# A streaming encoder trunk on one Trainium2 core: keys in plain fp32 and a divided norm in the opening

## The chip, the cores and the metric

The kernel runs on one core of a Trainium2 chip. Five engines work side by side, each with its own queue of instructions: TensorE (PE in the profile, and PEld for its loads of stationary weights), VectorE (DVE), ScalarE (ACT), GpSimd (POOL) and SyncE (SP), which here only issues transfers. The metric is the device time of one execution in microseconds (us); a kernel's time is the median of several runs.

## What is computed

One step of an encoder layer with 512 prompt positions and 8 x 16 sample positions, 640 rows of 1024 channels in all. Cut to what the change touches:

```python
xp = layer_norm(x_prompt, ln_in_g, ln_in_b)          # the same for x_sample
mem_k = mem_prompt @ w_mem_k                          # (256, 512): output, and keys of the prompt's attention
mem_v = mem_prompt @ w_mem_v                          # (256, 512): output, and values
z = x @ w_in                                          # 6656 columns: five inputs of three branches
...                                                   # branches a (conv + RG-LRU), b (conv), c (attention)
merged = g0 * out_a + g1 * out_b + g2 * out_c
x = layer_norm(alpha * x + merged @ w_out, ln1_g, ln1_b)
x = layer_norm(alpha * x + ffn(x), ln2_g, ln2_b)
```

All data are float32. `layer_norm` subtracts the row's mean, divides by its standard deviation, multiplies by a weight (g) and adds a bias (b) per channel.

## The kernel before, in words

**Products.** A float32 operand is split into a high part in the type fp32r (a copy on ACT, into tiles named `xh`, `wh`) and the rest (a subtraction on DVE, `xl`, `wl`). A product is then three fp32r matmuls: high x high, high x low, low x high. `split`, lines 199 to 201, does one operand, `split_all`, 203 to 208, several, all copies first. Activations stand turned, channels on partitions: `xh` and `xl` are [128, 8, 640].

**Order.** Everything is unrolled in program order. A list of `Step`s (257 to 303) holds a load of weights, the matmuls and what follows them. The loop at 1865 to 1893 takes them in order: it issues the high copies of the weights one step ahead at the start and two later (`prep_hi`), then the step's matmuls; at each `yield` in these, `advance` (319) lets side jobs, the generators in `streams`, issue instructions while a running sum of estimated prices says that ACT and DVE are ahead of PE, and after it come the waiting evacuations (`flush`, 310) and the low parts of the new weights (`prep_lo`). Each engine does its instructions strictly in that order, so a late one holds up those behind it. Scratch rows on chip are 53 slots, given out in the order in which they came free (`Slots`, 110). PSUM has four single banks (`pu`) and two double ones (`pv`).

**The opening.** Loads go out on SP's queue at lines 427 to 438: memory, key weights, x tile 0, gain and bias of the input norm repeated over 128 rows (`gb_in`, 1 MB), value weights, x tiles 1 and 2; line 1848 on adds x tiles 3 and 4, the first two loads of `w_in` and the rows of parameters (`pa`, `pb`, line 611). PE begins with warm-up matmuls on an identity (`idle`, 560 to 562). Then come eight steps (`mem_steps`, 589), four for the keys and four for the values, each with its half of the memory and one pair of weight blocks, all split. The dictionary `jobs` (584) writes out by hand what is issued after each: the memory's splits (`mem_split`), and for x tiles 0 to 3 statistics (`x_stats`), the norm in four DVE passes over rows (`x_norm`, 521), the turn by eight PE transposes into one `pv` (`x_turn`), the split out of PSUM and the store of the normed rows to the DRAM scratch `xn` (`x_split`, 533). `start_stream` (543) does tile 4 and the last two turns while the first product with `w_in` runs.

**The first product with `w_in`.** Its first three steps are a group (line 667 on): first the columns 0 to 319 of all three, which need x tiles 0 to 2, then columns 320 to 639, which need all five. `fm` (638) issues, for each block of 128 channels, the three products one after the other. Before the second columns `start_over` (700) finishes the stream.

**Later.** Gated products, attention, the recurrent branch; then eight steps of `proj_a` (line 1515), and the product with `w_out`, before which `before_out` (1630) begins to load the normed rows back from `xn` on POOL's queue as the residual (`load_res`, 1543; `x1_sum`, 1560).

Of the kernel before, what the change touches and what calls it, by code (L numbers as in the profile page):

```python
# [11 lines left out]
OP = mybir.AluOpType  # L12
# [131 lines left out]
def trunk(ctx, tc, x_prompt, x_sample, mem_t, rows_a, rows_b, hist_b, cache_k, cache_v, ln_in_g, ln_in_b, w_in,  # L144
# [251 lines left out]
    pa = one.tile([128, KD, 45], F32, name="pa")  # L396
# [3 lines left out]
    scratch = {n: tc.dram_tile([T, D], F32, name=n) for n in ("xn", "x1")}  # L400
# [80 lines left out]

    def to_xt(t, x):

        yield from room()
        p = pv()
        for c in range(2):
            for k in range(4):
                P.transpose(p[:, c, k * 128:(k + 1) * 128], x[c][:, k * 128:(k + 1) * 128], ident)
        yield None
        over()  # L490
        sl = slice(t * 128, (t + 1) * 128)
        split_all([(xh[:, 4 * c:4 * c + 4, sl], xl[:, 4 * c:4 * c + 4, sl], p[:, c].rearrange("p (k n) -> p k n", n=128))
                   for c in range(2)])
        turned.add(t)
        yield 1

# [21 lines left out]
    def x_root(t):  # L518
        norm[t] = ln_root(*norm[t])

    def x_norm(t):
        g, b = gb_in
        mv, ve, rs = norm.pop(t)
        y = xt[t]
        for c in range(2):
            V.scalar_tensor_tensor(y[c], y[c], mv[:, 0:1], g[c], op0=OP.subtract, op1=OP.mult)
            V.scalar_tensor_tensor(y[c], y[c], rs, b[c], op0=OP.mult, op1=OP.add)

    def x_turn(t):
# [13 lines left out]
    def start_stream():  # L543
        x_stats(4)
        yield None
        x_norm(4)
        for t in (3, 4):
            yield None
            yield from room()
            x_turn(t)  # L550
            yield None
            x_split(t)
        for r in gb_in:
            free(*r)

    def mem_end():
        stream("start", start_stream())
        P.time = max(P.time, V.time, A.time)
# [7 lines left out]
    def mem_evac(which):  # L566
# [6 lines left out]
        if which == "k":  # L573
            kv["k"] = out
        else:
            for m in range(2):
                hi, lo = get([128, 512], F32R), get([128, 512], F32R)
                split(hi, lo, out[m])
                vN[m] = (hi, lo)
            free(*out)  # L580
            for x in memT.values():
                free(*x)

    jobs = {0: [(mem_split, 1)], 1: [(mem_split, 2)], 2: [(mem_split, 3), (x_norm, 0)], 3: [(x_turn, 0), (x_stats, 1)],
            4: [(x_norm, 1), (x_split, 0), (mem_evac, "k"), (x_stats, 2)], 5: [(x_turn, 1), (x_norm, 2)],
            6: [(x_split, 1), (x_turn, 2), (x_stats, 3, False)],
            7: [(x_root, 3), (x_split, 2), (mem_evac, "v"), (x_norm, 3), (mem_end,)]}

    def mem_steps(which, li):
        for s in range(4):  # L590
            def mm(w, s=s):
# [12 lines left out]
            Step(mem_w[li + s], lambda r: r, [128, 2, 512], mm)  # L604
# [62 lines left out]
    def x_step(ld, o, evac, group=None):  # L667

        def mm(w):
# [4 lines left out]
            if group[1][0] is s:  # L674
                until(lambda: {0, 1, 2} <= turned)
                for z, q in enumerate(group[1]):
# [3 lines left out]
                    for n, few in enumerate(fm(q.p, q.w, xrh, xrl, KD, (0,))):  # L680
# [828 lines left out]
    for j in range(KD):  # L1509
# [4 lines left out]
                for j in range(0, KD, 2)])  # L1514
    proj_steps(0, proj_a, 8, aT, lambda: (sums_over(), finish("lru", "a")))
# [460 lines left out]
```

## Time and profile before

| | us |
|---|---|
| median of 3 runs | 1067.08 (1066.94 to 1067.94) |
| the profiled execution | 1068.33 |
| its span, first to last instruction | 1066.6 |
| PE busy in the span | 1045.3 |
| DVE busy | 799.8 |
| ACT busy | 486.0 |
| POOL busy | 86.1 |

The span is what the engines' records cover; the execution's own time is 1.73 us longer. An engine's busy time leaves out register, semaphore and DMA-issuing instructions. The mean granted clock of PE over the span is 0.994 of full speed. In lists of instructions a line starts with the start and the length in us, then engine, source line, operation, output and inputs by the program's names with the shape, the count of merged instructions, and in brackets the idle time before and what ended it. A plain fp32 matmul leaves two records.

### The profile page before, as it was taken

The page shows a single profiled execution, that of the slowest core. Times are in us where ns is not written, and L with a number is a line of the kernel's source. Part 1 is how long each engine was busy: PE and PEld are TensorE (multiplying, and loading weights), DVE is VectorE, ACT ScalarE, POOL GpSimd, SP SyncE. Part 2 cuts the span into 40 slices and gives each one's busy share as a digit, 9 for nine tenths or more (in the row PEclk, how much of TensorE's full clock was granted, in tenths as well). Part 3 has the DMA queues.
Part 4 walks back from the last instruction along what each step waited for, and adds up shares of the span by engine and source line. Part 5 has one row for each costly group of instructions (what it writes and reads, how often), then busy time and mean ns, then how long its engine had stood idle before and what let it go on. Part 6 is the DMA issues. An engine that isn't in the chain of part 4 may idle for free.

```text
span 1066.6 us, 16778 instructions
## 1 busy us (share of the span) xinstructions
PE 1045.3 (98%) x6745; PEld 996.2 (93%) x6745; DVE 799.8 (75%) x1383; ACT 486.0 (46%) x870; POOL 86.1 (8%) x140
## 2 busy tenths in 40 slices
PE   9899999999999999999999999999999999999997
PEld 8799899999999999999999889999999999888886
DVE  7939889889676745889645568888888887576775
ACT  5322545344675448656422355434444444444341
POOL 0100303231200000000000120000000000100111
PEclk9899999999999999999999999999999999999999
DMA  9822116531121222202323231222222222834471
GB/s 335 294 87 79 49 55 222 194 119 61 59 80 60 80 80 79 80 35 91 119 96 140 101 119 60 80 80 100 99 80 80 79 80 98 319 127 148 177 275 42
DMA packets 28511, 123.65 MB, mean 116 GB/s; under 512 B 3696, under 2 KB 4528, under 8 KB 18576
## 3 DMA queue, kind: packets, MB, share of 16 engines
q1 hardware_dynamic: 21744, 100.63, 26.5%
q0 software_dynamic: 6688, 21.94, 5.8%
q8 instruction: 53, 0.87, 0.3%
q14 instruction: 26, 0.21, 0.1%
HBM read 112.68 MB, written 9.88 MB: 115 GB/s over the span
## 4 chain that ended last, share of the span: by engine, by line
PE 84%; DVE 10%; DMA 3%; ACT 2%; issue 1%; POOL 0%; SPq 0%; DVEq 0%; ACTq 0%; POOLq 0%
PE pu L64 74%; PE pv L64 10%; DVE s L64 6%; DVE wl L64 2%; ACT s L64 1%; DMA s<-in_w_mem_k 1%; DMA s<-in_x_prompt 1%; DMA pb<-in_rows_b 1%; ACT L64 1%; DMA s<-in_w_mem_v 1%; DVE xres L64 0%; DVE mx L64 0%; DVE xl L64 0%; POOL s L781 0%; ACT wh L64 0%
## 5 line engine op out<-in xcount | busy, mean ns | idle before, releaser
L64 PE MATMUL pu<-xh,wh 128*128 128x320 f32 x1040 | 250.2, 313 | 4.2 <-ACT s L64 2.6
L64 PE MATMUL pu<-xh,wl 128*128 128x320 f32 x1040 | 247.5, 311 | 0.1
L64 ACT ACTIVATE wh<-wr 128x1024 fp32r<-128x1024 f32 (+1 forms) x149 | 135.0, 908 | 233.9 <-PE pu L64 141.1
L64 PE MATMUL pu<-xl,wh 128*128 128x320 f32 x888 | 220.1, 311 | 4.6 <-DVE xl L64 4.6
L64 PE MATMUL pu<-s,wh 128*128 128x320 f32 x1064 | 185.4, 310 | 1.8 <-DVE s L64 1.3
L64 PEld LDWEIGHTS pu<-xh,wh 128*128 128x128 f32 x1040 | 177.9, 190 | 8.5 <-ACT s L64 3.7
L64 PEld LDWEIGHTS pu<-xh,wl 128*128 128x128 f32 x1040 | 178.5, 190 | 0.3 <-ACT s L64 0.3
L64 DVE TENSOR_TENSOR wl<-wr,wh 128x1024 fp32r<-128x1024 f32 (+1 forms) x113 | 129.8, 1151 | 59.6 <-ACT wh L64 59.4
L64 DVE TENSOR_TENSOR s<-s,s 128x640 fp32r<-128x640 f32 (+4 forms) x180 | 128.8, 733 | 53.6 <-ACT s L64 51.5
L64 PEld LDWEIGHTS pu<-s,wh 128*128 128x128 f32 x1064 | 163.1, 188 | 3.2 <-ACT wh L64 1.1
L64 PEld LDWEIGHTS pu<-xl,wh 128*128 128x128 f32 x888 | 154.6, 190 | 5.4 <-DVE xl L64 5.4
L64 PE MATMUL pu<-s,wl 128*128 128x320 f32 x808 | 146.6, 309 | 0.0
L64 DVE TENSOR_TENSOR s<-s,pu 128x320 f32<-128x320 f32 x188 | 88.4, 484 | 72.1 <-PE pu L64 68.5
L64 ACT ACTIVATE s<-s 128x640 fp32r<-128x640 f32 (+4 forms) x148 | 90.0, 627 | 91.2 <-DVE s L64 90.0
L64 PEld LDWEIGHTS pu<-s,wl 128*128 128x128 f32 x808 | 125.5, 188 | 0.2 <-issue 0.2
L64 DVE SCALAR_TENSOR_TENSOR s<-s,pb,s 128x511 f32<-128x511 f32 (+14 forms) x240 | 114.5, 550 | 9.4 <-ACT s L64 9.4
L64 PE MATMUL pu<-wh,s 128*128 128x512 f32 (+1 forms) x396 | 114.6, 382 | 0.0
L64 PEld LDWEIGHTS pu<-wh,s 128*128 128x128 f32 x396 | 72.9, 188 | 14.1
L64 ACT ACTIVATE s<-pu 128x320 f32<-128x320 f32 (+2 forms) x90 | 36.6, 440 | 66.7 <-PE pu L64 66.7
L64 PE MATMUL pu<-wl,s 128*128 128x512 f32 (+1 forms) x198 | 61.6, 383 | 0.8 <-DVE wl L64 0.8
L64 PE MATMUL pv<-wh,s 128*128 128x512 f32 (+1 forms) x152 | 48.7, 367 | 0.4 <-DVE xres L64 0.4
L64 PE MATMUL pu<-s,s 128*128 128x512 f32 (+1 forms) x204 | 47.2, 382 | 0.0
(127 smaller groups left out, 1133.3 us busy)
## 6 DMA issues: line engine op xcount, KB each, us to landing
wr<-in_w_in SPq DMA_DIRECT2D x26, 1024.0 KB, 4.8
wr<-in_w_ffn_down SPq DMA_DIRECT2D x19, 1024.0 KB, 4.9
wr<-in_w_ffn_gate SPq DMA_DIRECT2D x11, 1024.0 KB, 4.8
wr<-in_w_ffn_up SPq DMA_DIRECT2D x11, 1024.0 KB, 4.7
s<-in_cache_k POOLq DMA_DIRECT2D x16, 256.0 KB, 5.7
s<-in_cache_v POOLq DMA_DIRECT2D x16, 256.0 KB, 5.1
wr<-in_proj_a SPq DMA_DIRECT2D x4, 1024.0 KB, 4.7
wr<-in_w_out SPq DMA_DIRECT2D x4, 1024.0 KB, 5.2
```

The lines of the kernel that those rows point to most:

```text
L64: return f(*a, **k)
```

## The change

Five things change together.

1. The keys are computed by plain fp32 matmuls of the unsplit memory and weights. The memory is still split for the values. The two runs of 15 warm-up matmuls become one of 10.
2. The input norm is divided. On rows, ACT scales by 1/deviation and shifts by -mean/deviation (`x_scale`). After the turn, where channels lie on partitions, weight and bias (two new columns of `pa`) are applied out of PSUM into slots, half of the eight blocks by ACT, half by DVE (`x_gain`); the split reads those slots. A turn takes two `pv` where both are free.
3. The order written out by hand is new. Tiles 3 and 4 are done at set places within the group by `start_work`; the split of the values goes to its end.
4. In the group's first and third step the first columns go by product (`apart`): eight matmuls high x high, eight high x low, eight low x high.
5. The rows stored in the opening are the unweighted ones (scratch `n`). `xn_stream`, added at the third step of `proj_a`, loads them and gain and bias on POOL's queue, multiplies and adds on DVE, and stores `xn`.

The diff, cut to its core:

```diff
-    scratch = {n: tc.dram_tile([T, D], F32, name=n) for n in ("xn", "x1")}
+    scratch = {n: tc.dram_tile([T, D], F32, name=n) for n in ("n", "xn", "x1")}
...
         mem_w.append(Blocks(w_mem_k, i))
+        if i < 2:
+            load_x(i)
         if i == 1:
-            load_x(0)
-    gb_in = load_gb(ln_in_g, ln_in_b, S)
+            S.dma_start(pa, rows_a.rearrange("p (k r) -> p k r", k=KD))
+    load_x(2)
     mem_w.append(Blocks(w_mem_v, 0))
-    load_x(1)
-    mem_w += [Blocks(w_mem_v, 1), Blocks(w_mem_v, 2)]
-    load_x(2)
-    mem_w.append(Blocks(w_mem_v, 3))
+    mem_w += [Blocks(w_mem_v, i) for i in range(1, 4)]
...
+    def x_scale(t):
+        mv, ve, rs, *shift = norm.pop(t)
+        ln_scale(xt[t], mv, rs, *shift)
         for c in range(2):
-            V.scalar_tensor_tensor(y[c], y[c], mv[:, 0:1], g[c], op0=OP.subtract, op1=OP.mult)
-            V.scalar_tensor_tensor(y[c], y[c], rs, b[c], op0=OP.mult, op1=OP.add)
+            S.dma_start(scratch["n"][t * 128:(t + 1) * 128, c * 512:(c + 1) * 512], xt[t][c])

     def x_turn(t):
-        turning[t] = to_xt(t, xt[t])
-        next(turning[t])
+        p = [pv() for _ in range(1 if side[0] else 2)]
+        turning[t] = [p[0][:, 0], p[-1][:, 2 - len(p)]]
+        side.append(len(p))
+        for c in range(2):
+            for k in range(4):
+                P.transpose(turning[t][c][:, k * 128:(k + 1) * 128], xt[t][c][:, k * 128:(k + 1) * 128], ident)
+
+    def x_gain(t):
+        free(*xt[t])
+        xt[t] = [get([128, 4, 128]) for _ in range(2)]
+        for k in range(KD):
+            src, to = turning[t][k // 4][:, k % 4 * 128:(k % 4 + 1) * 128], xt[t][k // 4][:, k % 4]
+            if k < 4:
+                A.activation(to, src, AF.Identity, scale=pa[:, k, 45:46], bias=pa[:, k, 46:47])
+            else:
+                V.tensor_scalar(to, src, pa[:, k, 45:46], pa[:, k, 46:47], op0=OP.mult, op1=OP.add)
+        over(side.pop())
...
-    idle(15)
-    mem_split(0)
-    idle(15)
+    idle(10)
...
-    jobs = {0: [(mem_split, 1)], 1: [(mem_split, 2)], 2: [(mem_split, 3), (x_norm, 0)], 3: [(x_turn, 0), (x_stats, 1)],
-            4: [(x_norm, 1), (x_split, 0), (mem_evac, "k"), (x_stats, 2)], 5: [(x_turn, 1), (x_norm, 2)],
-            6: [(x_split, 1), (x_turn, 2), (x_stats, 3, False)],
-            7: [(x_root, 3), (x_split, 2), (mem_evac, "v"), (x_norm, 3), (mem_end,)]}
+    jobs = {0: [(mem_split, 0), (x_stats, 0), (mem_split, 1), (x_scale, 0)], 1: [(x_stats, 1), (mem_split, 2), (x_scale, 1)],
+            2: [(x_turn, 0), (mem_split, 3), (x_stats, 2)], 3: [(x_gain, 0), (x_split, 0), (x_scale, 2)],
+            4: [(x_turn, 1), (x_gain, 1)], 5: [(x_turn, 2), (x_split, 1), (mem_evac, "k"), (x_gain, 2)],
+            6: [(x_split, 2)], 7: [(mem_evac, "v"), (x_stats, 3), (x_scale, 3), (x_stats, 4)]}
...
+                if which == "k":
                     for k in (2 * s, 2 * s + 1):
                         for m in range(2):
+                            P.matmul(p[m], mem[s][:, k % 2, m * 128:(m + 1) * 128], mem_w[s].tile[k % 2], start=(k == 0),
+                                     stop=(k == KD - 1))
+                    mem_w[s].take()
...
+        if apart:
+            for a, b in ((hi, rh), (hi, rl), (lo, rh)):
+                for k in range(K):
+                    for c in cs:
+                        P.matmul(p[c][:, :HT], a[:, k], b(k, c), start=(k == 0 and a is hi and b is rh),
+                                 stop=(k == K - 1 and a is lo))
+                yield b is rl
+            return
...
+    start_jobs = {0: [(x_shift, 4)], 5: [(x_turn, 3), (x_gain, 3), (x_scale, 4)], 6: [(x_split, 3)], 8: [(x_turn, 4)],
+                  9: [(x_gain, 4), (x_split, 4)], 10: [(values_stored,)]}
...
+    def xn_stream():
+        g, b = load_gb(ln_in_g, ln_in_b, G)
+        y = {t: [get([128, 512]) for _ in range(2)] for t in range(5)}
+        for t in range(5):
+            for c in range(2):
+                G.dma_start(y[t][c], scratch["n"][t * 128:(t + 1) * 128, c * 512:(c + 1) * 512])
+        for _ in range(4):
+            yield None
+        for t in range(5):
+            for c in range(2):
+                V.tensor_mul(y[t][c], y[t][c], g[c])
+                V.tensor_add(y[t][c], y[t][c], b[c])
+                G.dma_start(scratch["xn"][t * 128:(t + 1) * 128, c * 512:(c + 1) * 512], y[t][c])
+                yield 1
+            free(*y[t])
+            yield None
+        free(*g, *b)
+
     def before_out():
         flush()
+        finish("xn")
...
+        if i == first["pa"] + 2:
+            stream("xn", xn_stream())
```

The keys of `start_jobs` count the yields within the group's first columns: 0 to 2 in the first step, 4 to 7 in the second, 8 to 10 in the third.

More of the change, by code (lines that the diff above doesn't have):

```diff
@@ L395, in trunk @@
     xl = one.tile([128, KD, T], F32R, name="xl", tag="xl")
-    pa = one.tile([128, KD, 45], F32, name="pa")
+    pa = one.tile([128, KD, 47], F32, name="pa")
     pb = one.tile([128, KC, 34], F32, name="pb")
@@ L458, in ln_root, with ln_shift, ln_scale @@
         return mv, ve, rs
-    def ln_scale(y, mv, rs):
+    def ln_shift(mv, rs):
         shift = small.tile([128, 1], F32, name="shift")
         V.scalar_tensor_tensor(shift, mv[:, 0:1], -1.0, rs, op0=OP.mult, op1=OP.mult)
+        return shift
+    def ln_scale(y, mv, rs, shift=None):
+        shift = shift or ln_shift(mv, rs)
         for x in y:
@@ L480, in trunk @@
     turned = set()
[L482 to L495, printed above, removed]
     memT = {}
@@ L541, in last_x @@
         load_x(4)
[L543 to L558, printed above, removed]
-    idle(15)
-    mem_split(0)
-    idle(15)
+    idle(10)
     mem_acc = {}
@@ L572, in mem_evac, with values_stored @@
             S.dma_start(dst[m * 128:(m + 1) * 128], out[m])
[L573 to L582, printed above, removed]
-    jobs = {0: [(mem_split, 1)], 1: [(mem_split, 2)], 2: [(mem_split, 3), (x_norm, 0)], 3: [(x_turn, 0), (x_stats, 1)],
-            4: [(x_norm, 1), (x_split, 0), (mem_evac, "k"), (x_stats, 2)], 5: [(x_turn, 1), (x_norm, 2)],
-            6: [(x_split, 1), (x_turn, 2), (x_stats, 3, False)],
-            7: [(x_root, 3), (x_split, 2), (mem_evac, "v"), (x_norm, 3), (mem_end,)]}
+        kv[which] = out
+    def values_stored():
+        for m in range(2):
+            hi, lo = get([128, 512], F32R), get([128, 512], F32R)
+            split(hi, lo, kv["v"][m])
+            vN[m] = (hi, lo)
+        free(*kv["v"])
+        for x in memT.values():
+            free(*x)
+    jobs = {0: [(mem_split, 0), (x_stats, 0), (mem_split, 1), (x_scale, 0)], 1: [(x_stats, 1), (mem_split, 2), (x_scale, 1)],
+            2: [(x_turn, 0), (mem_split, 3), (x_stats, 2)], 3: [(x_gain, 0), (x_split, 0), (x_scale, 2)],
+            4: [(x_turn, 1), (x_gain, 1)], 5: [(x_turn, 2), (x_split, 1), (mem_evac, "k"), (x_gain, 2)],
+            6: [(x_split, 2)], 7: [(mem_evac, "v"), (x_stats, 3), (x_scale, 3), (x_stats, 4)]}
     def mem_steps(which, li):
@@ L602, in mm @@
                     f(*a)
-            Step(mem_w[li + s], lambda r: r, [128, 2, 512], mm)
+            if which == "k":
+                Step(None, None, None, mm)
+            else:
+                Step(mem_w[li + s], lambda r: r, [128, 2, 512], mm)
     mem_steps("k", 0)
@@ L635, in lambda_rows, with fm @@
         G.tensor_tensor(lru8, acc, ml, op=OP.add)
-    def fm(p, w, rh, rl, K, cs=(0, 1)):
+    def fm(p, w, rh, rl, K, cs=(0, 1), apart=False):
         hi, lo = w
+        if apart:
[6 more added lines that the diff above has]
+            return
         for k in range(K):
@@ L679, in mm @@
                     q.p = pu() if z < 2 else halves_of(pv())
-                    for n, few in enumerate(fm(q.p, q.w, xrh, xrl, KD, (0,))):
+                    for n, few in enumerate(fm(q.p, q.w, xrh, xrl, KD, (0,), z in (0, 2))):
                         if len(group) > 2:
@@ L699, in trunk, with start_work @@
     first = {"glu": len(steps)}
-    def start_over():
-        finish("start")
-    group = (start_over, [])
+    start_jobs = {0: [(x_shift, 4)], 5: [(x_turn, 3), (x_gain, 3), (x_scale, 4)], 6: [(x_split, 3)], 8: [(x_turn, 4)],
+                  9: [(x_gain, 4), (x_split, 4)], 10: [(values_stored,)]}
+    def start_work(_, n):
+        for f, *a in start_jobs.get(n, ()):
+            f(*a)
+    group = (flush, [], start_work)
     up = {}
@@ L1514, in trunk @@
                 for j in range(0, KD, 2)])
+    first["pa"] = len(steps)
     proj_steps(0, proj_a, 8, aT, lambda: (sums_over(), finish("lru", "a")))
@@ L1849, in reach @@
         if i == 0:
-            x_stats(0)
-            pump(1)
             last_x()
```

27 lines of the change are left out of this document (13 added, 14 removed).

## The prediction, made before the changed kernel was run

> **What bounds the kernel now.** I read the page first, for which engine is full and where it is not.
>
> ```profile
> span 1066.6 us, 16778 instructions
> ...
> PE 1045.3 (98%) x6745; PEld 996.2 (93%) x6745; DVE 799.8 (75%) x1383; ACT 486.0 (46%) x870; POOL 86.1 (8%) x140
> ...
> PEclk9899999999999999999999999999999999999999
> ```
>
> TensorE (PE) works in 98% of the span, so a change pays only where PE stands still, runs at a lower clock, or is given less work. Its granted clock, in tenths, falls to 8 in the second of the 40 slices (26.7 to 53.3 us) and nowhere else. The change works there, so I cut the opening into stretches with the table by windows (busy time and instructions of each engine, then PE's granted clock, the DMA share and the rate), and after it list PE's own instructions in order of time, with the idle time before each.
>
> ```profile
> 1.40:5.40 4.00, 3.96 (x18) 3.96 (x19) 1.22 (x2) 2.08 (x4) 0.00 (x0) 1.00 0.79 242
> 5.40:10.25 4.85, 4.85 (x45) 4.85 (x43) 1.74 (x4) 2.41 (x4) 0.00 (x0) 1.00 0.96 331
> 10.25:37.20 26.95, 25.45 (x124) 20.34 (x122) 26.17 (x46) 14.26 (x25) 2.76 (x3) 1.00 1.03 389
> ...
> 40.80:48.00 7.20, 7.19 (x30) 7.19 (x31) 6.99 (x12) 0.00 (x0) 0.71 (x1) 0.58 0.93 282
> 48.00:57.70 9.70, 8.35 (x60) 7.87 (x58) 5.05 (x9) 2.17 (x4) 0.72 (x1) 1.00 0.31 117
> ```
>
> ```profile
> 1.45 9.05 PE L64 MATMUL pu<-ident 128*128 128x128 f32 x60 [1.45 <-DVE ident L64]
> ...
> 12.19 1.99 PE L64 MATMUL pu<-wh,s 128*128 128x512 f32 x8
> 14.01 1.07 PE L64 MATMUL pu<-wl,s 128*128 128x512 f32 x4
> ...
> 21.27 1.03 PE L64 MATMUL pv<-ident,s 128*128 128x128 f32 x8
> 22.06 1.17 PE L64 MATMUL pu<-wh,s 128*128 128x512 f32 x4
> ...
> 40.81 0.64 PE L64 MATMUL pu<-xl,wh 128*128 128x320 f32 x1 [3.34 <-DVE xl L64]
> ...
> 56.62 0.41 PE L64 MATMUL pu<-xh,wh 128*128 128x320 f32 x1 [0.69 <-ACT xh L64]
> 57.83 0.41 PE L64 MATMUL pu<-xl,wh 128*128 128x320 f32 x1 [0.80 <-DVE xl L64]
> ...
> 64.83 0.31 PE L64 MATMUL pv<-xh,wh 128*128 128x320 f32 x1
> ```
>
> The reader is to see four things. First, the 60 records of warm-up matmuls (30 calls, two records each) hold PE until 10.5. Second, from 10.25 to 37.2, keys and values with their turns, VectorE (DVE) is busy 26.17 of 26.95 us: PE is fed by DVE there. Third, at 40.81 PE has waited 3.34 us for `xl`, which DVE writes, and the next 7.2 us run at a mean clock of 0.58, 7.2 x 0.42 = 3.0 us lost. Fourth, the part of the first three `w_in` steps that needs the late rows (columns 320 to 639, "second half" below) starts at 56.62 and stops until 57.83; from there to 64.83 run the 47 matmuls left of the first two steps, 0.149 us each, which puts its undisturbed start at 57.83 - 0.15 = 57.7.
>
> PE's need up to there: 96 matmuls of 512 columns at (14.01 - 12.19) / 8 = 0.228 us, 21.8; five turns of eight transposes at 22.06 - 21.27 = 0.79 us, 4.0; 72 matmuls of 320 columns, 10.7. That is 36.5 of the 47.45 us from 10.25 to 57.7, so 10.9 are lost. After 57.7 PE has one larger wait, at 131, shown below. What is taken off the 57.7 is therefore taken off the end, unless a later stage gives it back.
>
> **The change part by part.** *Warm-up.* `idle(10)` in place of twice `idle(15)` leaves 10 of the 30 calls, all in the slow beginning: 1.40 to 5.40 holds 18 records, the next 4.85 us hold 45. Twenty records take until about 1.4 + 4.0 + 2 x 4.85/45 = 5.6. Then the keys may start, because they no longer wait for a split.
>
> *Keys in plain fp32.* 16 matmuls in place of 48. The nearest row is the only plain fp32 product of such width:
>
> ```profile
> 259.10 1.35 PE L64 MATMUL pv<-s,ones 128*128 128x512 f32 x4 [0.27 <-POOL s L781]
> 260.20 0.54 PE L64 MATMUL pu<-xh,wh 128*128 128x320 f32 x2
> ```
>
> 640 columns pass in 260.20 - 259.10 = 1.10 us, so 512 take 0.88, and 16 take 14.1 against 48 x 0.228 = 10.9: PE gets 3.2 us more. In return 8 copies of ScalarE (ACT) and 8 subtractions of DVE go, one pair for each half block of key weights. The splits of the memory stay, since the values use them.
>
> *Loads.* What the first matmuls wait for is the queue of loads; the chain of waits gives four landings (start and length of the transfer).
>
> ```profile
> 3.06 5.60 DMA s<-in_w_mem_k
> ...
> 8.67 5.39 DMA s<-in_w_mem_k
> ...
> 14.08 6.93 DMA s<-in_x_prompt
> ...
> 21.02 5.34 DMA s<-in_w_mem_v
> ```
>
> In program order these end 1.5, 3.5, 5.5 and 7.5 MB into the queue: landed at 8.7, 14.1, 21.0 and 26.4. The change takes out 1 MB of gain and bias rows and brings forward 0.18 MB (`pa`) and x. By the same positions the second key block (2.0 MB) lands at 10.0, the fourth (4.18) at 16.4, the first half of the value weights (4.93) at 19.0, its second (5.18) at 19.9, x tile 4 (7.68) at 26.8, the first two `w_in` loads at 29.5 and 32.2. The ten stores of rows on SP stay ten, now of the unweighted rows, and come behind all these loads, as before; the `w_in` loads after them have until their slot of 2 is free. Keys on PE, four matmuls a block, from 5.6: 9.1 when block 1's first half lands at 9.3, 12.8 when block 2's lands at 13.2; these 0.6 us of waits and the first turn put the end at 5.6 + 14.1 + 0.6 + 0.8 = 21.1.
>
> *Norm divided.* Per tile of x DVE loses four passes and gets four gains; ACT gets two scalings and four gains; the order is statistics, scaling, turn, gain, split. Rows (mean ns of one after the bar, or length and count):
>
> ```profile
> L64 DVE TENSOR_TENSOR wl<-wr,wh 128x1024 fp32r<-128x1024 f32 x97 | 118.1, 1220 | 53.1 <-ACT wh L64 52.9
> ...
> L64 DVE TENSOR_TENSOR s<-s,wr 128x512 f32<-128x512 f32 x48 | 33.0, 688 | 0.8
> ...
> L64 DVE SCALAR_TENSOR_TENSOR s<-s,rs,s 128x512 f32<-128x512 f32 x10 | 7.5, 751 | 0.7
> ```
>
> ```profile
> 20.94 1.28 DVE L64 BATCH_NORM_STATS2 st<-s 128x6 f32<-128x512 f32 x2
> ...
> 22.58 1.29 DVE L64 TENSOR_TENSOR wl<-s,wh 128x512 fp32r<-128x512 f32 x2
> ```
>
> ```profile
> 605.19 1.50 ACT L64 ACTIVATE s<-pv,pa 128x128 f32<-128x128 f32 x4 [1.83 <-PE pv L64]
> ...
> 614.99 1.52 ACT L64 ACTIVATE s<-s,shift,rs 128x512 f32<-128x512 f32 x2 [0.99 <-DVE shift L64]
> ```
>
> ```profile
> 24.81 2.21 ACT L64 ACTIVATE wh<-s 128x512 fp32r<-128x512 f32 x4
> ...
> 29.64 1.06 ACT L64 ACTIVATE wh<-wr 128x1024 fp32r<-128x1024 f32 x1
> ```
>
> ```profile
> 612.18 1.37 DVE L64 TENSOR_SCALAR s<-pv,pa 128x128 f32<-128x128 f32 x4
> ```
>
> ```profile
> 22.73 0.95 POOL L457 TENSOR_TENSOR rs<-ve,mhalf 128x1 f32<-128x1 f32 x1 [10.54 <-DVE ve L64]
> ```
>
> So on DVE 4 x 0.75 = 3.0 become 1.37 per tile; on ACT 1.52 + 1.50 = 3.0 are added. With eight key subtractions of 0.65 DVE loses 5.2 + 5 x 1.6 = 13.3 us; ACT loses 8 x 0.55 = 4.4 and gains 15. ACT takes DVE's place as the engine that feeds PE. I follow ACT's queue in its new order, because it is strictly in order. Value block 0, second half, 19.9 to 20.45; gains of tile 0 to 21.95; its split copies, the second behind DVE's gains, 23.05; scaling of tile 2 behind DVE's lower parts and shift, 23.8 to 25.3; then without a wait value block 1 (1.1), gains 1 (1.5), block 2 (1.1), split 1 (1.1), the key copies (1.1), gains 2 (1.5), block 3 (1.1), split 2 (1.1): 34.9. The first two `w_in` blocks (1.0 each) end at 35.9 and 36.9.
>
> PE beside it: value steps from 21.1, each when ACT and DVE have its block; the last starts at 33.25 and ends 12 x 0.228 later, 36.0. The first half of the group starts there: the new order (`apart`) needs only copies for its first eight matmuls, which is why no 3.34 us wait is left. The next price is tile 3: DVE ends the lower part of the second block at 38.3 (two of 1.22 after 35.9), statistics 1.64 (22.58 - 20.94 in the rows), POOL's power 0.95, shift: 41.0; ACT scales until 42.5. PE meets its turn after 36 matmuls, 36.0 + 5.4 = 41.4, and waits 1.1. Turn until 43.3, 12 matmuls until 45.1; ACT's third block, gains 3 and scaling 4 end at 43.5, 45.0, 46.5; eight matmuls until 46.3, wait 0.2, turn 4 until 47.3; 16 matmuls until 49.7. ACT meanwhile: split 3 until 47.6, gains 4 49.1, first copy 49.65, DVE's lower part 50.3. So the second half starts at 49.7 and stops once, undisturbed start 50.1. The split of the values, moved behind gains 4 (1.1 on ACT, 1.3 on DVE), lies beside PE's second half and has its first reader far behind it. The cover of each turn is now the matmuls around it; where ACT is 1 us later, PE is too.
>
> The saving is 57.7 - 50.1 = 7.6 us. The same by terms: PE begins 4.65 earlier (10.25 to 5.6), works 3.2 more, and loses 44.5 - 39.7 = 4.8 instead of 10.9: 4.65 - 3.2 + 6.1 = 7.55. The bounds: were PE never fed late after the keys, 21.1 + 10.9 + 4 x 0.79 + 10.7 = 45.9, a saving of 11.8; were loads the limit, only their 0.82 MB at (26.4 - 8.7) / 6 = 3.0 us per MB, 2.4. I take ACT's path, every duration of which has a row.
>
> *Clock.* The rows show when PE pays double: after 3.34 us of waiting, and here after 2.40.
>
> ```profile
> 131.00 0.74 PE L64 MATMUL pu<-xh,wh 128*128 128x320 f32 x2 [2.40 <-ACT s L64]
> ```
>
> ```profile
> 131.00:137.00 6.00, 6.00 (x30) 5.85 (x31) 6.00 (x15) 2.81 (x6) 0.00 (x0) 0.72 0.00 0
> ```
>
> After the 2.40 us, the mean clock of six us is 0.72: 6 x 0.28 = 1.7 more. My waits stay at 1.1 or under, so I count no spell. The Trainium skill ("TensorE: Matmul & The Clock Gate", part 1) puts the fall to half rate behind an idle window of about 3.4 us; by it the sum is the same, but rival (b) below would begin only at 3.4 us and be worth 0.04 at most. The row, with its 2.40, disagrees and decides.
>
> *Residual rows later.* Gain and bias of x now run in `xn_stream`, from the third `proj_a` step: 20 DVE passes of 0.69, 13.8 us, and on POOL's queue 14 loads and 10 stores. DVE there:
>
> ```profile
> 546.06 0.89 DVE L64 TENSOR_TENSOR s<-s,pu 128x320 f32<-128x320 f32 x2 [3.43 <-PE pu L64]
> ...
> 553.11 0.89 DVE L64 TENSOR_TENSOR s<-s,pu 128x320 f32<-128x320 f32 x2 [3.42 <-PE pu L64]
> ```
>
> DVE waits 3.42 us for PE in each step of 553.11 - 546.06 = 7.05, and a tile's four passes are 2.75. What a late pass delays is the evacuation behind it in the queue, whose PSUM is wanted two steps on, and `wl`, needed as late. Six steps give 20 us of room for 13.8. POOL has nothing else queued but the later residual loads, which had waited there for slots. I take 0; the ends are -0.5 (stores off the opening) and +13.8, all of it exposed. Everything else keeps its order, shifted.
>
> Sum: span 1066.6 - 7.6 = 1059.0; around it lie 1.7 (1068.33 of the profiled execution), 1060.7; the median 1067.08 is 1.25 under that execution: 1059.5.
>
> **The rivals.** (a) PE is not held up by ACT, because the semaphores let passes overlap more than my in-order sum: 11.8 saved, 1055.3. For it: ACT stands at 14.26 of 26.95 us now; against: its queue gets 15 us more. 0.13. (b) One wait in the group grows to 2.4 to 3.3 us, at tile 3's scaling, and brings a slow spell: 1.2 to 2.1 plus 1.7 to 3.0, so 7.6 - 4.0 = 3.6 saved, 1063.5. For it: DVE, POOL and ACT stand in line there. 0.12. (c) Loads bound the opening: 2.4 saved, 1064.7, at the edge of 0.2% and counted as no change. Against: the DMA share is 0.31 at 48 to 57.7, where PE still waits. 0.06. (d) The keys, fed in pieces by loads and with fewer warm-up calls, stay at half clock: 14.1 us more, of which the 0.6 of waits is covered. Then PE alone sets the pace, 45.9 + 13.5 = 59.4, a loss of 1.7: 1068.8, within 0.2%. 0.05. (e) Slower: the `xn` rows land late, DVE stands at its first pass in the in-order queue, evacuations and `wl` stand behind it, and PE runs dry. It decides from 7.6 + 2.1 exposed; at the full 13.8 the time is 1073.3. For it: the same POOL queue had waited for slots in that stretch. Against: 14 issues and a landing fit into the two steps that the stream lets pass. 0.09.
>
> **How the numbers follow.** 0.2% is 2.1 us, about what a measurement of this kernel can tell. My forecast has 0.55, with its own range 1057 to 1062: ACT's path 2.5 us longer or shorter. Faster: 0.55 + 0.13 + 0.12 = 0.80; same: (c) and (d), 0.11; slower: (e), 0.09. The range leaves out (d) and (e), and the far end of (a): 1054 to 1064.8. The low end is (a) and the 2.4 us wait at 131 shrinking with it.
>
> **What would show it.** In the profile after: 20 warm-up records; key matmuls at 0.43 per record of 512 columns from about 5.6; no wait of over 1.5 us before the second half, which starts near 50; clock 10 in the second slice; ACT over 80% busy from 20 to 50, DVE under 80%. PE without a gap through the `proj_a` steps, and `xn` passes in DVE's former waits. I am wrong if PE waits for key loads over 2.4 us, if the clock falls in the opening, or if PE waits for DVE behind `xn` rows.

## The result and the profile after

| | us |
|---|---|
| median after, 6 runs | 1058.98 (1058.07 to 1060.24) |
| median before, 6 runs beside them | 1067.01 (1064.95 to 1067.94) |
| ratio, with its 95% interval | 0.9927 (0.9914 to 0.9939) |
| the profiled execution after, its span | 1059.77, 1058.0 |

The change saves 8.0 us by the medians and 8.6 by the two profiled spans. First the page of the kernel after: engines with busy time, share of the span and instructions, then the granted clock in 40 slices.

```profile
span 1058.0 us, 16736 instructions
...
PE 1041.5 (98%) x6689; PEld 986.7 (93%) x6689; DVE 801.6 (76%) x1400; ACT 495.9 (47%) x892; POOL 96.0 (9%) x164
...
PEclk9999999999999999999999999999999999999999
```

The clock's 8 in the second slice is gone, and PE is busy 3.8 us less while the span is 8.6 shorter, so 4.8 us of standing still are gone too. The table by windows shows where. Its columns after the length are the busy time and instructions of PE, of its weight loads, DVE, ACT and POOL, then PE's clock, the DMA share and GB/s. The kernel before:

```profile
10.00:20.00 10.00, 10.00 (x48) 8.31 (x47) 9.80 (x18) 4.49 (x8) 0.87 (x1) 1.00 1.05 388
20.00:30.00 10.00, 9.56 (x51) 7.76 (x49) 9.55 (x19) 6.86 (x14) 1.21 (x2) 1.00 1.03 394
30.00:40.00 10.00, 6.42 (x29) 4.51 (x29) 9.79 (x16) 5.71 (x9) 2.15 (x2) 1.00 0.88 332
40.00:50.00 10.00, 9.19 (x44) 9.19 (x45) 9.69 (x17) 0.20 (x1) 1.44 (x1) 0.66 0.82 261
```

And the kernel after:

```profile
10.00:20.00 10.00, 10.00 (x31) 4.93 (x30) 6.60 (x15) 5.74 (x11) 1.09 (x2) 1.00 1.05 392
20.00:30.00 10.00, 10.00 (x52) 7.90 (x50) 7.80 (x19) 9.14 (x20) 0.00 (x0) 1.00 1.03 400
30.00:40.00 10.00, 10.00 (x58) 8.64 (x56) 8.61 (x16) 7.04 (x12) 0.54 (x1) 1.00 0.94 315
40.00:50.00 10.00, 9.02 (x61) 8.30 (x60) 7.61 (x18) 8.68 (x18) 0.54 (x1) 1.00 0.56 196
```

DVE, full before, now has 1.4 to 3.4 us free in each ten; ACT has gone from 6.86, 5.71 and 0.20 to 9.14, 7.04 and 8.68; PE runs without a gap from 10 to 40. PE's own instructions in order of time, after:

```profile
1.45 4.64 PE L64 MATMUL pu<-ident 128*128 128x128 f32 x20 [1.45 <-DVE ident L64]
5.88 11.11 PE L64 MATMUL pu<-s,s 128*128 128x512 f32 x24
...
20.73 1.49 PE L64 MATMUL pu<-wh,s 128*128 128x512 f32 x4
...
34.18 1.34 PE L64 MATMUL pu<-xh,wh 128*128 128x320 f32 x8
...
39.47 1.36 PE L64 MATMUL pv<-ident,s 128*128 128x128 f32 x8
...
47.09 0.41 PE L64 MATMUL pu<-xh,wh 128*128 128x320 f32 x1
48.43 0.41 PE L64 MATMUL pu<-xl,wh 128*128 128x320 f32 x1 [0.93 <-DVE xl L64]
```

Keys begin at 5.88, values at 20.73, the group's first columns at 34.18, the turn of tile 3 at 39.47, and the second half at 47.09, with one stop until 48.43. Its undisturbed start (the start after the stop less one matmul of 0.15, as in the prediction; called S below) is 48.28 against 57.68 before: 9.4 us saved. Later the two traces run in step. A stop of 0.75 us that came at 475.09 comes at 465.75, 9.3 earlier; the gap is still 9.3 behind `proj_a` and 8.6 at the end. Of that last 0.7, 0.3 is one wait: at 990.80 PE waits 0.67 us for DVE's `xres`, where before it waited 0.38 for it, at 999.60. The rest comes in small pieces and is not explained; the six runs of one kernel differ by more.

### The profile page after: what moved, and what is told of

Read it like the earlier page. It is cut to its first block, busy times and chain, and to the rows that moved or that the text cites. A ratio compares the mean times of both kernels' runs of the same rounds, so it can differ in the third digit from the quotient of the medians.

```text
span 1058.0 us, 16736 instructions
## 1 busy us (share of the span) xinstructions
PE 1041.5 (98%) x6689; PEld 986.7 (93%) x6689; DVE 801.6 (76%) x1400; ACT 495.9 (47%) x892; POOL 96.0 (9%) x164
## 4 chain that ended last, share of the span: by engine, by line
PE 83%; DVE 9%; ACT 3%; DMA 2%; issue 1%; POOL 0%; SPq 0%; DVEq 0%; ACTq 0%; POOLq 0%
PE pu L64 73%; PE pv L64 9%; DVE s L64 7%; ACT s L64 2%; DVE wl L64 1%; ACT L64 1%; DMA s<-in_w_mem_k 1%; DMA n<-s 1%; DMA s<-in_w_mem_v 1%; DVE xres L64 0%; ACT wh L64 0%; DMA s<-in_x_prompt 0%; DVE mx L64 0%; POOL s L784 0%; DVE xl L64 0%
## 5 line engine op out<-in xcount | busy, mean ns | idle before, releaser
L64 PE MATMUL pu<-xh,wh 128*128 128x320 f32 x1040 | 246.9, 312 | 3.5 <-ACT s L64 2.6
L64 PE MATMUL pu<-xh,wl 128*128 128x320 f32 x1040 | 244.3, 310 | 0.0
L64 PE MATMUL pu<-xl,wh 128*128 128x320 f32 x888 | 216.6, 310 | 1.4 <-DVE xl L64 1.4
L64 DVE TENSOR_TENSOR s<-s,s 128x640 f32<-128x640 f32 (+5 forms) x200 | 141.8, 728 | 57.1 <-ACT s L64 54.8
L64 PE MATMUL pu<-wh,s 128*128 128x512 f32 x364 | 107.0, 383 | 0.0
L64 PEld LDWEIGHTS pu<-wh,s 128*128 128x128 f32 x364 | 66.9, 188 | 13.8 <-ACT wh L64 0.6
L64 PE MATMUL pu<-s,s 128*128 128x512 f32 (+1 forms) x236 | 61.9, 413 | 0.0
L64 PE MATMUL pu<-wl,s 128*128 128x512 f32 x182 | 57.1, 381 | 0.0
L64 PEld LDWEIGHTS pu<-s,s 128*128 128x128 f32 x236 | 43.1, 190 | 14.1 <-issue 7.1
```

Of the source, the lines that this page charges most:

```text
L64: return f(*a, **k)
```

## The experiments

All but one start from the kernel after; times with a ratio are medians over several runs, the rest are one execution. S is as above.

| what is different | S | span | time | ratio to before (95%) |
|---|---|---|---|---|
| before | 57.68 | 1066.6 | 1067.01 | 1 |
| after | 48.28 | 1058.0 | 1058.98 | 0.9927 (0.9914 to 0.9939) |
| before + plain keys | 55.59 | 1064.6 | 1065.98 | 0.9996 (0.9985 to 1.0006) |
| keys split again | 55.94 | 1065.3 | 1067.61 | 1.0010 (0.9999 to 1.0020) |
| norm whole again | 51.53 | 1060.9 | 1062.98 | 0.9965 (0.9953 to 0.9977) |
| 1 MB more to load | 52.61 | 1060.8 | 1062.56 | |
| no order by product | 47.89 | 1057.6 | 1059.72 | 0.9943 (0.9925 to 0.9961) |
| no `xn` rows | 48.41 | 1057.8 | 1059.22 | 0.9920 (0.9904 to 0.9937) |
| 30 warm-up calls | 52.16 | 1061.9 | 1063.65 | |
| 1 warm-up call | 48.19 | 1056.6 | 1058.38 | |
| all gains on ACT | 55.07 | 1066.3 | 1068.30 | |
| tile 3 earlier | 48.23 | 1058.0 | 1059.74 | |
| the same, second half by product | | 1056.6 | 1059.49 | 0.9928 (0.9914 to 0.9941) |
| evacuation first, later on | 47.60 | 1053.5 | 1056.18 | 0.9901 (0.9886 to 0.9915) |

Span less S is 1008.2 to 1009.8 in all but two: 1011.2 with all gains on ACT, and 1005.9 in the last row, whose edit lies in a later stage. In the others what happens in the opening arrives at the end within 1.6 us.

**Keys alone.** To the kernel before, only the plain keys and the ten warm-up calls are added.

```diff
-    idle(15)
+    idle(10)
...
-    idle(15)
...
+                if which == "k":
...
+                            P.matmul(p[m], mem[s][:, k % 2, m * 128:(m + 1) * 128], mem_w[s].tile[k % 2], start=(k == 0),
+                                     stop=(k == KD - 1))
```

> The kernel before with only the plain fp32 keys and 10 warm-up matmuls; loads, norm and hand-written order as before. Theory F (in-order queues of DVE and ACT feed PE; the change frees them): PE starts its keys near 6 in place of 10.25, DVE loses 8 subtractions of 0.65, but still has the norm's 20 passes, so the second half's undisturbed start moves from 57.7 to 52 to 54, and a wait of over 2 us on DVE with a slow spell after it stays; time 1062 to 1063.5. Rival L (loads bound the opening): loads are unchanged, so 57 to 58 and 1067. Rival K (the keys are the whole gain): 49 and 1059.

S came 2.1 us earlier, less than expected; the ratio cannot be told from 1. PE's row and the windows of this kernel:

```profile
38.77 0.64 PE L64 MATMUL pu<-xl,wh 128*128 128x320 f32 x1 [3.36 <-DVE xl L64]
```

```profile
30.00:40.00 10.00, 5.91 (x28) 4.51 (x27) 9.90 (x17) 5.21 (x8) 1.47 (x1) 0.89 0.87 315
40.00:50.00 10.00, 10.00 (x57) 9.99 (x57) 8.91 (x14) 0.53 (x2) 1.44 (x1) 0.77 0.80 264
```

DVE is still full (9.90 of 10), PE still waits 3.36 us for its lower part, and the clock falls to 0.77 after it. The earlier start of PE is mostly given back in that wait.

**Keys split again.** The kernel after with the keys as before, and the memory's first split ahead of them.

```diff
-                if which == "k":
...
+                for a, b in ((0, 0), (0, 1), (1, 0)):
...
+            Step(mem_w[li + s], lambda r: r, [128, 2, 512], mm)
```

> The changed kernel with the keys split again into three fp32r products, the rest of the change kept. F: ACT gets 8 copies of 0.55 and DVE 8 subtractions of 0.65 back, PE gets 3.2 us less; the second half starts at 50 to 52 (48.3 after), time 1061 to 1063. L: 48.3, no change. K: 57, 1067.

The whole gain is gone, more than expected. PE's rows, and the windows:

```profile
17.06 1.81 PE L64 MATMUL pu<-wh,s 128*128 128x512 f32 x4 [3.39 <-ACT s L64]
...
32.07 1.25 PE L64 MATMUL pu<-wh,s 128*128 128x512 f32 x4 [1.94 <-ACT wh L64]
```

```profile
10.00:20.00 10.00, 6.00 (x20) 4.52 (x21) 6.54 (x15) 3.64 (x7) 0.95 (x2) 0.87 1.05 392
30.00:40.00 10.00, 7.91 (x38) 5.96 (x37) 7.34 (x16) 10.00 (x22) 0.00 (x0) 1.00 0.67 247
```

Here PE waits for ACT (3.39 with a fall of the clock to 0.87, later 1.94). From 30 to 40 ACT is busy 10.00 of 10 us. From 10 to 20 it is busy only 3.64: the copy of the memory that PE waits for until 17.06 stands in ACT's queue behind the scaling of tile 0, and that stands until DVE has made the shift.

```profile
13.93 1.52 ACT L64 ACTIVATE s<-s,shift,rs 128x512 f32<-128x512 f32 x2 [3.37 <-DVE shift L64]
```

So ACT's in-order queue is the bound, in part by the amount of its work, with the copies of the keys on top of the divided norm, and in part by the order of this kernel. An order made for split keys was not tried, so the price of the split alone is not shown. The two halves of the change do not add: keys alone take 2.1 off S, everything but the keys 57.68 - 55.94 = 1.7, both together 9.4. Each alone leaves a bound standing: DVE's work in the first, ACT's queue in the second.

**Norm whole again.** The norm in four DVE passes on rows, weight and bias of x loaded in the opening, no `xn_stream`; plain keys, order by product and the new order stay.

```diff
+            gb_in = load_gb(ln_in_g, ln_in_b, S)
...
-        ln_scale(xt[t], mv, rs, *shift)
+            V.scalar_tensor_tensor(y[c], y[c], mv[:, 0:1], g[c], op0=OP.subtract, op1=OP.mult)
+            V.scalar_tensor_tensor(y[c], y[c], rs, b[c], op0=OP.mult, op1=OP.add)
```

> The changed kernel with the norm whole on rows again: four DVE passes per tile, gain and bias rows loaded (1 MB) in the opening, the split out of PSUM, the normed rows stored in the opening, no later stream. F: DVE gets about 1.6 us per tile back and is the feeder again; the second half starts at 53 to 56, time 1063.5 to 1066.5. L: only the 1 MB counts, 2.4 to 2.7 us, 51. K: 48 to 49.

S is 51.53, 3.25 later than after: short of the 53 to 56 expected, and near the 51 of rival L, by which only the megabyte counts. PE's longest wait in it:

```profile
15.34 3.70 PE L64 MATMUL pu<-s,s 128*128 128x512 f32 x8 [1.99 <-DMA s<-in_w_mem_k]
```

It is for a load of key weights; waits for DVE stay at 0.56 to 0.77. So PE's longest wait is not for DVE's passes, although DVE is at 9.79 of 10 us from 20 to 30.

**The load alone.** The kernel after, and 1 MB of gain and bias rows loaded at the same place, ahead of the last two key blocks, and read by nobody.

```diff
         if i == 1:
+            gb_in = load_gb(ln_in_g, ln_in_b, S)
             S.dma_start(pa, rows_a.rearrange("p (k r) -> p k r", k=KD))
```

> The changed kernel with the 1 MB of gain and bias rows loaded again in the opening, ahead of the value weights; nobody reads them. F: the value weights land about 2.7 us later, ACT's chain had waited 1.9 us for them, so the second half starts 1.5 to 2.7 us later, at 50 to 51. L: the saving of 9.4 us is the loads': 55 to 57.

```profile
16.18 5.36 PE L64 MATMUL pu<-s,s 128*128 128x512 f32 x8 [3.25 <-DMA s<-in_w_mem_k]
```

```profile
10.00:20.00 10.00, 6.75 (x12) 2.65 (x11) 3.44 (x8) 3.69 (x6) 0.55 (x1) 0.83 1.05 374
```

S is 4.3 us later, more than expected, and less than by rival L. PE waits 3.25, and its mean clock over ten us is 0.83; ACT's first copy of the value weights starts at 20.91 in place of 17.51, 3.4 later, and its gains of tile 1 then wait 0.79 for PE's turn. The 3.25 us that the norm on rows lost are thus no more than such a load costs by itself. With this megabyte in the opening S is 51.53 with the norm whole and 52.61 with the norm divided (one trace each, and the landing alone moves S by up to 0.7 between runs): these runs show no gain from dividing it as work. What they show is that the divided norm lets the load leave the opening. What dividing is worth without the load they do not say, since a whole norm needs the rows. Before, this megabyte stood behind all key blocks, so its price there may be smaller.

**Order by product.** The group's first columns go block by block again.

```diff
-                    for n, few in enumerate(fm(q.p, q.w, xrh, xrl, KD, (0,), z in (0, 2))):
+                    for n, few in enumerate(fm(q.p, q.w, xrh, xrl, KD, (0,), False)):
```

> The changed kernel with the group's three products block by block as before, nothing else. F: PE waits at the start of the first half for the first block's low parts, 0.7 to 1.5 us, of which the later wait for tile 3 takes back about half; second half at 48.5 to 49.5, time 1059 to 1060.5. Rival A (the order by product is what removed the 3.34 us wait and its slow spell): 3 to 6 us later, 1062 to 1065.

A wait of 0.38 appears at 34.66, less than the 0.7 to 1.5 expected, and S is 0.4 earlier than after: the order by product gains nothing that can be measured, and rival A falls. That no 3.34 us wait is left is not the work of this order; the lower parts now come in time.

**No `xn` rows.** The residual reads the unweighted rows; this kernel leaves out weight and bias of the input norm in the residual, and with them the stream's passes, loads and stores.

```diff
-            G.dma_start(res[t][c], scratch["xn"][t * 128:(t + 1) * 128, c * 512:(c + 1) * 512])
+            G.dma_start(res[t][c], scratch["n"][t * 128:(t + 1) * 128, c * 512:(c + 1) * 512])
...
-            stream("xn", xn_stream())
```

> The changed kernel without the later stream: the residual of the first norm is read from the unweighted rows, so gain and bias of the input norm are left out of the residual. F: the 20 DVE passes and 24 transfers lie in DVE's waits for PE, time as after within 0.5 us, PE without another gap between 470 and 600. Rival E (the stream costs something in the proj_a steps): 1 to 3 us faster than after.

1059.22 against 1058.98: the stream costs nothing that these runs can tell. The trace after shows why; these are DVE's rows in a `proj_a` step.

```profile
546.58 3.48 DVE L64 TENSOR_TENSOR s<-s,s 128x512 f32<-128x512 f32 x5
550.82 0.89 DVE L64 TENSOR_TENSOR s<-s,pu 128x320 f32<-128x320 f32 x2 [0.77 <-PE pu L64]
```

Four of the five merged passes are a tile of the stream, 2.75 us; the fifth is the step's own, which stood there before. They lie in what had been a wait of 3.42 us, of which 0.77 is left, and PE has no gap there.

**30 warm-up calls, and 1.** PE starts later or earlier, everything else the same.

```diff
-    idle(10)
+    idle(30)
```

> The changed kernel with 30 warm-up matmuls as before. PE starts the keys 4.4 us later, near 10.3. If ACT's queue sets the pace of the values (as the prediction had it), about 1.5 us of it reach the second half: 50. If PE itself sets the pace, 4 us or more: 52 to 53. Between: 51.

> The changed kernel with one warm-up matmul in place of ten. If the clock opens after some 4 us of PE work of whatever kind, the plain fp32 keys warm it themselves: they start when the first weights land, near 4.3 in place of 5.9, and what of that they lose at half rate leaves 0.5 to 1.3 us; second half at 47 to 47.8 (48.3 after), time 1058. Rival D (fed in pieces by loads, the keys stay at half clock): they end over 5 us later, second half beyond 53, 1064 or more.

PE's rows with 30 calls:

```profile
10.62 10.47 PE L64 MATMUL pu<-s,s 128*128 128x512 f32 x24
...
52.31 0.42 PE L64 MATMUL pu<-xl,wh 128*128 128x320 f32 x1 [0.92 <-DVE xl L64]
```

The keys start 10.62 - 5.88 = 4.7 us later, and S is 3.9 later. By the expectation this would mean that PE itself sets the pace. But the run does not tell the two engines apart, because ACT's gains read what PE has turned:

```profile
21.56 1.50 ACT L64 ACTIVATE s<-pv,pa 128x128 f32<-128x128 f32 x4 [3.09 <-PE pv L64]
...
28.64 1.50 ACT L64 ACTIVATE s<-pv,pa 128x128 f32<-128x128 f32 x4 [0.92 <-PE pv L64]
...
36.51 2.05 ACT L64 ACTIVATE wh<-wr 128x1024 fp32r<-128x1024 f32 x2
```

ACT stands 3.09 and 0.92 us for these turns, waits that the kernel after does not have, and starts its copies for `w_in` 36.51 - 32.64 = 3.87 later, which is the delay of S. Had ACT been free for these gains only at 20.45, as the prediction had it, it would have stood 21.56 - 20.45 = 1.1 there, by this estimate. With one call:

```profile
4.75 12.02 PE L64 MATMUL pu<-s,s 128*128 128x512 f32 x24 [2.50 <-DMA s<-in_w_mem_k]
```

The keys start 1.1 earlier, after a wait for their load, but their first records run at the slow rate: the first 24 end at about the same time, values start 0.2 earlier and S is 0.1 earlier, not the 0.5 to 1.3 expected. PE's slow beginning is paid either in warm-up calls or in keys.

Which engine sets the pace shows when the starts of both are put beside S, in us, for the kernel after and the five that leave the loads and ACT's order in the opening as they are:

| kernel | values start on PE | ACT's first copy of the value weights | ACT's first copy for `w_in` | S |
|---|---|---|---|---|
| after | 20.73 | 17.51 | 32.64 | 48.28 |
| no order by product | 19.93 | 17.12 | 32.26 | 47.89 |
| no `xn` rows | 20.42 | 17.64 | 32.77 | 48.41 |
| 1 warm-up call | 20.51 | 17.40 | 32.55 | 48.19 |
| evacuation first, later on | 19.74 | 16.82 | 31.96 | 47.60 |
| 30 warm-up calls | 24.83 | 17.15 | 36.51 | 52.16 |

In the first five rows S lies 30.77 to 30.79 behind ACT's first copy of the value weights, and 27.55 to 27.99 behind PE's start of the values: S follows ACT, and with it the passes of DVE that ACT waits for. From ACT's first copy for `w_in` it is 15.63 to 15.65 in all six. ACT itself waits there for the value weights to land (1.92 to 1.93 us in each), so a landing that comes 0.7 earlier by nothing in the opening's code, as in the fifth row, shows as 0.7 at S. That PE has no gap from 10 to 40 does not speak against it: from the values to the group PE takes 34.18 - 20.73 = 13.45 us in the kernel after and 33.54 - 19.74 = 13.80 in the fifth row, where it starts 1.0 earlier, and of the 0.35 more only 0.15 is a gap in the records.

**All gains on ACT.** The four gains of a tile that DVE does go to ACT.

```diff
-            if k < 4:
+            if k < 8:
```

> The changed kernel with all eight gains of a tile on ACT in place of four there and four on DVE. If ACT's in-order queue feeds PE, its path gets 1.4 us per tile: the second half starts 4 to 6 us later, at 52 to 54. If PE sets the pace: under 1.5 us later, 48.3 to 49.8.

```profile
35.41 2.02 PE L64 MATMUL pu<-wh,s 128*128 128x512 f32 x4 [2.74 <-ACT wh L64]
```

```profile
18.82 2.88 ACT L64 ACTIVATE s<-pv,pa 128x128 f32<-128x128 f32 x8
```

```profile
20.00:30.00 10.00, 8.83 (x45) 6.63 (x43) 3.10 (x6) 9.09 (x22) 0.00 (x0) 1.00 1.03 401
30.00:40.00 10.00, 7.26 (x25) 5.47 (x24) 6.66 (x10) 8.98 (x20) 0.00 (x0) 0.83 0.71 265
```

DVE falls to 3.10 and 6.66 of 10 us, ACT is at 9.09 and 8.98, PE waits 2.74 for it and the clock falls to 0.83. S is 6.8 later, past the 52 to 54 expected, and the time is that of before. A tile's gains take ACT 2.88 us in place of 1.49 (at 18.71 in the kernel after, shown below), 7.0 us more for five tiles, and 6.8 of them arrive at S. So ACT's queue has nothing to spare in the kernel after: it sets the pace, and the four gains on DVE keep it as short as it is.

**Tile 3 earlier.** In the kernel after ACT stands 2.96 us before it can scale tile 3:

```profile
17.51 1.29 ACT L64 ACTIVATE wh<-s 128x512 fp32r<-128x512 f32 x2 [1.93 <-DMA s<-in_w_mem_v]
18.71 1.49 ACT L64 ACTIVATE s<-pv,pa 128x128 f32<-128x128 f32 x4
...
32.64 2.03 ACT L64 ACTIVATE wh<-wr 128x1024 fp32r<-128x1024 f32 x2
...
38.60 1.52 ACT L64 ACTIVATE s<-s,shift,rs 128x512 f32<-128x512 f32 x2 [2.96 <-DVE shift L64]
```

Its statistics were put ahead of the split of tile 2, its scaling ahead of the evacuation of the values; in a second kernel the second half's first step also goes by product.

```diff
-            6: [(x_split, 2)], 7: [(mem_evac, "v"), (x_stats, 3), (x_scale, 3), (x_stats, 4)]}
+            6: [(x_stats, 3), (x_split, 2)], 7: [(x_scale, 3), (mem_evac, "v"), (x_stats, 4)]}
...
-            yield from fm(s.p, w, xrh, xrl, KD, (1,))
+            yield from fm(s.p, w, xrh, xrl, KD, (1,), first["glu"] == state["i"])
```

> The changed kernel with the statistics of tile 3 moved from after to before the low parts of the first two w_in blocks, and its scaling ahead of the value copies. If what is left of the waits in the group is DVE's and ACT's order (the shift of tile 3 had kept ACT waiting 2.96 us), the turn of tile 3 comes at 39.5 without a wait and the second half starts 0.8 to 1.6 us earlier, 46.7 to 47.5. If it is the amount of ACT's work: 48.0 to 48.5.

> The same as a_early, and the second half of the group's first step also goes by product, so that its first eight matmuls need no low parts of tile 4. The stop of 0.93 us before the second half goes too: undisturbed start 46.0 to 47.0, time 1056.5 to 1058, 0.1 to 0.2% below the changed kernel. If ACT's amount of work is the limit: 47.5 and 1058.5.

S moved by 0.05 in the first, to what the rival gave (48.0 to 48.5), and the second's ratio, 0.9928, is that of the kernel after. Both missed what was expected. But ACT's wait was not taken away; these are its rows in the first:

```profile
37.57 1.52 ACT L64 ACTIVATE s<-s,shift,rs 128x512 f32<-128x512 f32 x2 [3.08 <-DVE shift L64]
...
39.96 1.05 ACT L64 ACTIVATE wh<-wr 128x1024 fp32r<-128x1024 f32 x1
```

DVE makes the shift of tile 3 behind its two lower parts for `w_in`, as before, so ACT still stands 3.08 us, and its third `w_in` copy starts at 39.96 where it started at 40.03. What removing the wait would bring stays open. With order by product in the second half its stop is another one, 0.54 us for ACT's `xh` at 49.06, and the first matmul into `pv` behind it, at 55.62, is no earlier than the 55.43 of the kernel after; ACT's first copy of the value weights was 0.4 later in this run, at 17.95.

**The evacuation first, later on.** The largest wait left in the kernel after is at 121.60. PE's row, ACT's rows and the window behind it:

```profile
121.60 0.74 PE L64 MATMUL pu<-xh,wh 128*128 128x320 f32 x2 [2.42 <-ACT s L64]
```

```profile
119.23 0.48 ACT L64 ACTIVATE s<-pv,nm 128x256 f32<-128x256 f32 x1
...
119.81 1.28 ACT L64 ACT_TABLE_LOAD   x1
121.11 0.77 ACT L64 ACTIVATE s<-pu 128x320 f32<-128x320 f32 x2
```

```profile
120.00:125.00 5.00, 3.40 (x16) 3.26 (x17) 5.00 (x12) 4.39 (x8) 0.00 (x0) 0.82 0.01 3
125.00:130.00 5.00, 5.00 (x35) 5.00 (x35) 4.66 (x11) 1.41 (x5) 1.07 (x2) 0.84 0.02 9
```

PE wants a PSUM bank that ACT evacuates at 121.11, and ACT does that behind the attention's exponentials and a load of its function tables, because the side jobs (`advance`) are handed out ahead of the waiting evacuations (`flush`). In this one step they are handed out after them.

```diff
+            if i == first["glu"] + 10:
+                flush()
             advance()
             flush()
```

> The kernel after, with the evacuations that stand in the queue handed out before the attention's four exponentials in the one step of the main loop in which ScalarE's Sigmoid evacuation stood behind eight exponentials (the wait of 2.42 us of TensorE at 121.60 in the profile after). Nothing is left out. If that wait costs its own 2.42 us and the half-clock spell behind it (about 1.7 us more), both go: span about 1054, median about 1055, ratio to the kernel before 0.989, and no clock figure below 1 near 120 to 135. Rival: ScalarE then loads its tables once more (1.28 us each) and the wait comes back a step later, in the same or another size: 1058 to 1059.5, ratio 0.992 to 0.993. Neither theory expects a change before 115.

ACT's rows and PE's largest wait near there, in this kernel:

```profile
112.73 1.28 ACT L64 ACT_TABLE_LOAD   x1
114.03 0.77 ACT L64 ACTIVATE s<-pu 128x320 f32<-128x320 f32 x2
...
120.03 1.28 ACT L64 ACT_TABLE_LOAD   x1 [3.47 <-issue]
```

```profile
131.98 1.06 PE L64 MATMUL pv<-ident,s 128*128 128x128 f32 x8 [0.61 <-DVE s L64]
```

```profile
120.00:125.00 5.00, 5.00 (x36) 5.00 (x35) 5.00 (x12) 4.17 (x10) 0.00 (x0) 1.00 0.01 3
```

The evacuation runs at 114.03, the table loads have moved and not multiplied, the clock stays at 1.00, and a wait of 0.61 is left, at 131.98. At 110 this trace is 0.7 ahead of the kernel after, at the wait of 289.78 (now 285.59) 4.2: 3.5 us gained of the 4.1 expected, the 0.6 being the new wait. By medians it is 2.8, the ratio's interval (0.9886 to 0.9915) only touches that of the kernel after (0.9914 to 0.9939), and all five runs (1055.24 to 1056.30) are faster than the fastest of the kernel after. This is the fastest version.

## Why the prediction was right, step by step

The forecast was 1059.5 and its reason holds: PE starts earlier, DVE's queue is shorter, and ACT's queue in its new order sets the pace up to the second half. Several sizes were off. That the forecast lies only 0.5 from the median is in part luck: S came 50.1 - 48.28 = 1.8 earlier than forecast, 0.8 of the saving was given back by the end, and the profiled execution lay 0.8 above its median where 1.25 had been taken.

- **Warm-up, keys.** Forecast: keys from 5.6, 14.1 us of PE, 0.6 of waits for loads, end at 21.1. Measured: from 5.88, 20.73 - 5.88 - 0.79 for the turn = 14.06, no wait, end at 20.73. The price from the one plain fp32 row was right.
- **Landings.** Forecast for the first block of value weights: 19.0 and 19.9. ACT waited for it until 17.51, and its two copies ran on without a break, so the second half was there by 18.2. This was the largest error, and nearly all of the 1.8 by which S was early. A part: the queue moved 263 and 367 GB/s in the first two stretches where before it moved 242 and 331, 0.26 MB or 0.7 us more by 10.25; the rest comes from placing landings by position between four rows.
- **ACT's path.** Forecast: split of tile 2 done at 34.9, `w_in` blocks at 35.9 and 36.9. Measured: 32.64 and 34.67. It began 1.5 to 1.7 earlier, with the landing, and ended 2.2 earlier. From the gains of tile 0 to the `w_in` copies it took 32.64 - 18.71 = 13.9 us, where 34.9 - 20.45 = 14.45 were forecast. "ACT takes DVE's place as the engine that feeds PE" held: S keeps its distance to ACT's first copy of the value weights within 0.02 us in five kernels, and 7.0 us more work on ACT made S 6.8 later. PE is close to its own pace all the same, as only 2.75 of the 4.8 us forecast as lost remain: from 5.88 to 48.28 are 42.4 us, and PE's need is the 36.5 of before with 14.06 for the keys in place of 10.9, 39.65. Rival (a), PE not held up by ACT, did not come about.
- **Tile 3.** Forecast: POOL's power 0.95, scaling at 41.0, a wait of 1.1 for the turn. Measured: 0.54, 38.60, and no wait, since the turn follows the 36th matmul directly.

```profile
37.83 0.54 POOL L456 TENSOR_TENSOR rs<-ve,mhalf 128x1 f32<-128x1 f32 x1 [19.25 <-DVE ve L64]
```

- **Second half.** Forecast: from 49.7 with a stop until 50.3. Measured: 47.09, stop until 48.43. By terms: start 4.4 earlier (4.65 forecast), work 3.15 more (3.2), losses 10.9 to 2.75 (to 4.8): 9.4 saved instead of 7.6.
- **Clock, `xn` stream.** No spell and no cost were forecast, and there were none; ACT is busy 83% of 20 to 50 and DVE 80%, where over and under 80% had been named.
- **Later.** Not foreseen: of the 9.4 us 8.6 are left at the end of the span, 0.3 of the rest by the longer wait for `xres`. And the changed `fm` also orders the FFN's group by product, which the prediction passed over; the gap between the traces shrinks by 0.04 across it.
- **Rivals.** Loads as the bound (c) did not come about, but a megabyte put back costs 4.3: that the gain and bias rows left the opening is a condition of the gain. Of rival (b) there is no sign in the trace after, (d) did not come about even with one warm-up call, and (e) not by the kernel without `xn` rows.

## What to carry to other kernels

When the bound of a stretch is an engine that feeds another, list the queues that stand just behind it before pricing a change: plain keys alone, or everything but the plain keys, were worth about 2 us each, and 9.4 together. To learn which engine sets the pace, delay the suspected one by a known time and see how much of the delay arrives at the end, but look also whether the delay makes its rival wait: 30 warm-up calls delayed PE and, through the turns, ACT. Small differences in start between kernels that are otherwise alike tell as much: the end follows the engine that sets the pace. And look at the order in which side jobs and evacuations are handed to an in-order engine: two lines there gave a further 2.8 us.

## What the runs showed of the hardware

- **The clock falls after shorter waits than a rule says.** Waits of PE of 2.42, 2.74, 3.25, 3.36 and 3.39 us were each followed by a fall of the granted clock, to 0.77 to 0.89 in the mean of the windows that hold it; waits of 1.94 and 1.99 were not (1.00). With the 2.40 of the kernel before, the edge here lies between 1.99 and 2.40. The Trainium skill ("TensorE: Matmul & The Clock Gate", part 1) puts it at an idle window of about 3.4 us; the first three of these waits disagree. The spell after the 2.42 cost 5 x 0.18 + 5 x 0.16 = 1.7 us beyond the wait.
- **The slow beginning has no fixed length.** The same 20 warm-up records took 3.94 to 4.64 us from run to run, so the keys start up to 0.7 earlier or later, by nothing in the kernel. The granted clock reads 1.00 there, although records come at half the later rate.
- **POOL's power of 128 values** took 0.54 to 0.55 us in this opening and 0.87 to 1.47 before, where DVE was full; the runs don't show that one causes the other.
